# Moving the DRAM-to-DRAM copies of a strided slice to the gpsimd queue and dealing the loads to the sync and scalar queues

## Chip, cores and metric

The kernel runs on one core of one Trainium2 chip. The metric is the device time of one execution in microseconds (us), the median of several runs; less is better. A core has 16 DMA engines, which move all the data here. The engines that issue DMAs are SP (sync), ACT (scalar) and POOL (gpsimd); no engine computes anything in this kernel.

## The reference

The reference takes an array `x` of 32 batches, each 1024 rows of 512 float32 numbers, and returns every second row of the first 512 rows of each batch.

```python
batch, seq, dim = 32, 1024, 512
x = np.random.randn(batch, seq, dim).astype(np.float32)
start, stop, stride = 0, 512, 2
...
return x[:, start:stop:stride, :].astype(np.float32)
```

A row is 2,048 bytes. The result has 32 x 256 rows, so 16.78 MB are read from HBM and 16.78 MB are written to it.

## The kernel before, in words

The 256 output rows of a batch are split by parity: the 128 rows with an even number and the 128 with an odd number (`two`, line 14, gives one parity of two batches as a pattern of 128 x 2 x 512). One parity of each batch is copied straight from `x` to `out`, DRAM to DRAM; the other is loaded into an SBUF tile, `held` (128 partitions x 32 batches x 512 numbers), and stored from there. `apart` (line 8) says which parity of a batch goes the direct way: it is 1 for batches 0, 1, 4, 5 of a group of eight and 0 for batches 2, 3, 6, 7.

The batches are taken in four groups of eight (`groups`, line 30). For each group the loop at lines 36 to 41 issues four loads on SP (line 40) and four direct copies on ACT (line 41), by turns. A load takes two neighbouring batches, 512 KB. A direct copy takes two batches of the group that have the same parity (steps of 5 or 3 apart), 512 KB also. The values of `apart` make the load and the copy of one turn of the loop take opposite parities. Every load of a group adds 16 to that group's own semaphore, `loaded[g]`, when it has landed; every copy adds 16 to `done[1]`.

After all 16 loads, SP goes on with the stores (lines 42 to 46): for each group it waits until the four loads of the group have landed (line 43), then issues eight stores, one for each batch, 256 KB each (line 46), which add to `done[0]`. Last, SP waits for all 32 stores and all 16 copies (lines 47 and 48), and the kernel ends.

So SP's queue holds 16 loads and behind them 32 stores, ACT's queue holds 16 copies, and POOL issues no DMA. Nothing in the program orders the copies against the loads or stores; the order in a queue is the order of issue. There is no planner.

Of the kernel before, what the change touches and what calls it, by code (L numbers as in the profile page):

```python
# [3 lines left out]

EIGHT = 8


def apart(b):


    return 1 - (b >> 1 & 1)


def two(t, b, step, parity):

    return t[b : b + step + 1 : step].rearrange("b (p two) d -> two p b d", two=2)[parity]


def kernel(tc, x, start, stop, stride, out):

    nc = tc.nc
    src = x[:, start:stop:stride, :]
    B, rows, D = out.shape
    P = rows // 2
    sp, act = nc.sync, nc.scalar
    groups = range(0, B, EIGHT)  # L30
    with tc.tile_pool(name="io", bufs=1) as io:
        held = io.tile([P, B, D], x.dtype, name="held")
        with tc.tile_critical():
            loaded = [nc.alloc_semaphore(name=f"loaded{g}") for g in groups]
            done = [nc.alloc_semaphore(name=f"done{i}") for i in range(2)]
            for g in groups:
                for i, (b, step) in enumerate(((0, 5), (2, 5), (1, 3), (3, 3))):
                    b += g
                    at = g + 2 * i
                    sp.dma_start(held[:, at : at + 2], two(src, at, 1, 1 - apart(at))).then_inc(loaded[g // EIGHT], 16)  # L40
                    act.dma_start(two(out, b, step, apart(b)), two(src, b, step, apart(b))).then_inc(done[1], 16)
            for g in groups:
                sp.wait_ge(loaded[g // EIGHT], 16 * 4)
                for b in range(g, g + EIGHT):
                    to = out[b].rearrange("(p two) d -> two p d", two=2)[1 - apart(b)]
                    sp.dma_start(to, held[:, b]).then_inc(done[0], 16)
            sp.wait_ge(done[0], 16 * B)
            sp.wait_ge(done[1], 16 * (B // 2))


# [1 line left out]
_INS = ['x', 'start', 'stop', 'stride']  # L52
_OUTS = [((32, 256, 512), 'float32')]

_NUMBERS = {'start': 0, 'stop': 512, 'stride': 2}


def kernel(**inputs):
    import numpy as _np
    import concourse.bacc as _bacc  # L60
    import concourse.tile as _tile
    from concourse import mybir as _mybir
    from concourse.bass_utils import run_bass_kernel_spmd as _run

    nc = _bacc.Bacc("TRN2", target_bir_lowering=False, num_devices=1)  # L65
    arrays, args = {}, []
    for name in _INS:
        if name in _NUMBERS:
            args.append(_NUMBERS[name])
            continue  # L70
        a = _np.ascontiguousarray(inputs[name])
        if a.dtype.kind in "iu":
            a = a.astype(_np.int64)
        arrays[f"in_{name}_dram"] = a
        args.append(nc.dram_tensor(f"in_{name}_dram", a.shape, _mybir.dt.from_np(a.dtype), kind="ExternalInput").ap())
    for i, (shape, dtype) in enumerate(_OUTS):
        dt = _mybir.dt.from_np(_np.dtype(dtype))
        args.append(nc.dram_tensor(f"out_{i}_dram", shape, dt, kind="ExternalOutput").ap())
    with _tile.TileContext(nc) as tc:
        kernel(tc, *args)  # L80
    r = _run(nc, [arrays], core_ids=[0])
    got = tuple(r.results[0][f"out_{i}_dram"] for i in range(len(_OUTS)))
    return got[0]
```

## Time and profile before

| | |
|---|---|
| Median of 4 runs | 81.31 us (81.17 to 81.41) |
| The profiled execution's own time | 81.28 us |
| Its span, first to last instruction | 79.5 us |
| Loads on SP | 16 x 512 KB, 8.39 MB |
| Direct copies on ACT | 16 x 512 KB, 8.39 MB |
| Stores on SP | 32 x 256 KB, 8.39 MB |
| Bytes that the DMA engines moved | 25.17 MB, mean 317 GB/s |
| Busy time of the compute engines | POOL 0.2 us, four memsets of the program's frame |

The table's byte counts take a direct copy once, although it reads HBM and writes HBM. In the profile, q1 is SP's queue and q10 is ACT's: their bytes are those of loads plus stores, and of copies. A DMA packet of 2,048 bytes is one row on one of the 16 DMA engines; packets of 4 bytes are the semaphore updates that end a DMA on each engine. "Landing" is when the last of these updates has arrived. A view can be cut to a window of time, in us from the start of the span.

### The profile page before, as it was taken

How to read it: one execution, taken by the hardware profiler on the slowest of the kernel's cores; microseconds unless marked ns; L12 is line 12 of the kernel's file. 1: busy time of each engine (PE TensorE's matmuls, PEld its weight loads, DVE VectorE, ACT ScalarE, POOL GpSimd, SP SyncE). 2: the span in 40 equal slices, each digit the busy share in tenths (PEclk: the TensorE clock that was granted, in tenths of full speed). 3: DMA queues.
4: the chain of work that ended last, by engine and by line, in shares of the span. 5: the costliest groups of instructions: out<-in, count | busy, mean ns of one | idle time of the engine just before them, and what ended most of it. 6: DMA issues, size and time to landing. Idle time of an engine off the chain costs nothing. (4 is left out here: it accounts for less than half of the span.)

```text
span 79.5 us, 115 instructions
## 1 busy us (share of the span) xinstructions
POOL 0.2 (0%) x4
## 2 busy tenths in 40 slices
POOL 1000000000000000000000000000000000000000
DMA  0899989999999999999999999989999999999980
GB/s 0 250 311 279 282 257 351 339 341 373 326 322 366 352 332 310 299 292 304 364 356 341 355 349 308 301 239 406 407 403 389 351 346 361 344 362 362 347 277 9
DMA packets 13312, 25.17 MB, mean 317 GB/s; under 512 B 1024, under 2 KB 1024, under 8 KB 13312
## 3 DMA queue, kind: packets, MB, share of 16 engines
q1 hardware_dynamic: 8960, 16.78, 64.0%
q10 hardware_dynamic: 4352, 8.39, 32.6%
HBM read 16.78 MB, written 16.78 MB: 422 GB/s over the span
## 5 line engine op out<-in xcount | busy, mean ns | idle before, releaser
L65 POOL MEMSET const-bfloat16-1.0<- 128x1 bf16 x1 | 0.1, 101 | 0.0
L65 POOL MEMSET const-uint8-127<- 128x1 uint8 x1 | 0.1, 101 | 0.0
L65 POOL MEMSET const-float32-0.0<- 128x1 f32 x1 | 0.1, 98 | 0.2 <-issue 0.2
L65 POOL MEMSET const-float32-1.0<- 128x1 f32 x1 | 0.1, 98 | 0.0
## 6 DMA issues: line engine op xcount, KB each, us to landing
out_dram<-in_x_dram ACTq DMA_DIRECT2D x16, 512.0 KB, 22.2
held<-in_x_dram SPq DMA_DIRECT2D x16, 512.0 KB, 22.3
out_dram<-held SPq DMA_DIRECT2D x32, 256.0 KB, 10.1
```

The costliest lines, as they stand in the source:

```text
L65: nc = _bacc.Bacc("TRN2", target_bir_lowering=False, num_devices=1)
```

## The change

The direct copies are issued by POOL (`nc.gpsimd`) in place of ACT. The loads are dealt by turns to SP and ACT: the first and third of each group on SP, the second and fourth on ACT, eight on each queue in all. The stores stay on SP with their waits as they were, now behind eight loads in place of 16. Sizes, patterns, semaphores and the number of DMAs are the same.

```diff
-    sp, act = nc.sync, nc.scalar
+    sp, act, pool = nc.sync, nc.scalar, nc.gpsimd
...
                     at = g + 2 * i
-                    sp.dma_start(held[:, at : at + 2], two(src, at, 1, 1 - apart(at))).then_inc(loaded[g // EIGHT], 16)
-                    act.dma_start(two(out, b, step, apart(b)), two(src, b, step, apart(b))).then_inc(done[1], 16)
+                    to = held[:, at : at + 2]
+                    (sp, act)[i % 2].dma_start(to, two(src, at, 1, 1 - apart(at))).then_inc(loaded[g // EIGHT], 16)
+                    pool.dma_start(two(out, b, step, apart(b)), two(src, b, step, apart(b))).then_inc(done[1], 16)
```

## Prediction before the run

> **What bounds the kernel now.** I read the page first, for who is busy.
>
> ```profile
> span 79.5 us, 115 instructions
> ...
> DMA  0899989999999999999999999989999999999980
> GB/s 0 250 311 279 282 257 351 339 341 373 326 322 366 352 332 310 299 292 304 364 356 341 355 349 308 301 239 406 407 403 389 351 346 361 344 362 362 347 277 9
> ...
> q1 hardware_dynamic: 8960, 16.78, 64.0%
> q10 hardware_dynamic: 4352, 8.39, 32.6%
> HBM read 16.78 MB, written 16.78 MB: 422 GB/s over the span
> ...
> out_dram<-in_x_dram ACTq DMA_DIRECT2D x16, 512.0 KB, 22.2
> held<-in_x_dram SPq DMA_DIRECT2D x16, 512.0 KB, 22.3
> out_dram<-held SPq DMA_DIRECT2D x32, 256.0 KB, 10.1
> ```
>
> All 16 DMA engines are busy from 2 us to 77 us, and a DMA lands 10 to 22 us after its issue: it stands in line. So the issuing of DMAs is not the bound; the time is bytes over rate. But the rate isn't constant: about 320, then four slices at 389 to 407, then about 350. I cut the time at those places and asked for the windows (columns: window, its length, POOL's busy time and count, clock, DMA share, GB/s).
>
> ```profile
> 2.00:53.50 51.50, 0.00 (x0) 1.00 1.01 319
> 53.50:56.00 2.50, 0.00 (x0) 1.00 1.05 403
> 56.00:60.50 4.50, 0.00 (x0) 1.00 1.05 406
> 60.50:76.50 16.00, 0.00 (x0) 1.00 1.06 354
> ```
>
> The engines are equally busy in all four, so the slow windows are made of longer packets, not of gaps. Next, the queues' shares in the first window, and then in the first microsecond of the second.
>
> ```profile
> q1 hardware_dynamic: 4342, 8.39, 51.9%
> q10 hardware_dynamic: 4169, 8.05, 48.7%
> ```
>
> ```profile
> q10 hardware_dynamic: 103, 0.20, 52.7%
> q1 hardware_dynamic: 106, 0.19, 50.5%
> ```
>
> In the first, loads (q1) and copies (q10) share the engines equally; nearly every byte there is read from HBM, at 319 GB/s. In the second, copies still hold half, but q1 has gone from loads to stores (the last load was issued at 31.2 us and landed 23.4 us later, at 54.6; its bulk was over by 53.5): half of the bytes are read from HBM, all are written to it, and the rate is 403. The packet records say the same: before 53.5 a 2,048-byte packet usually takes 84 ns, but about one in thirteen takes 100 ns or more, up to 1,000 and over; from 53.5 to 60 all take 84, copies' too. From 60.5 on, with stores alone, about half take 90 to 150.
>
> So what costs time is reading at full rate. Copies beside stores ran at the engines' own rate; copies beside loads did not. Before, all reading is done first (16.4 MB, 51.5 us) and one half of the writing, the stores, is left over for a stage that reads nothing.
>
> **What the Trainium skill says.** "DMA: Bandwidth & Descriptors", section "Issuing engines are not separate DMA queues": DMAs of all issuing engines run on the same 16 engines, and using more engines saves only issue time. The trace agrees that issue time is not wanted. Its section "Queues, rings and completion order": each DMA engine takes its queues in turn, packet by packet. The 51.9% and 48.7% agree for two queues. Its section "SWDGE vs HWDGE vs iDMA": a DMA from GpSimd has its descriptors made by software on that engine and kept in SBUF, with a packet preferably up to 4,096 bytes; its "Latency and other measured facts" gives about 1 us to the first byte against 0.6, and says that DMA engines 7 and 15 are usually slower, perhaps because of these rings. No DMA in this trace is of that kind, so nothing here confirms it.
>
> **The change part by part.** Bytes, packets and semaphores stay the same: 8.39 MB each of loads, copies and stores.
>
> *Dealing the loads to two queues.* SP issued its loads unhindered up to the eighth (16 issues took 33.06 us because the queue was full). With eight loads each, SP and ACT issue theirs in 6 to 8 us and SP reaches the first wait. Behind the wait on SP are only stores. Issue time: nothing, hidden by the queued transfers; without that cover, eight issues of 0.4 to 2.0 us.
>
> *A third queue.* With three queues in turn the copies have a third of the engines while loads run, in place of a half. The loads end earlier, and a part of the copies is left to run beside stores. The first group's four loads are 2.1 MB, at two thirds of 319 GB/s some 10 us after the first packet, so SP's waits end long before its queue reaches stores: nothing waits there.
>
> Stage 1, loads and a third of copies: 8.39 / (2/3) = 12.58 MB, nearly all reads, at 319 GB/s: 39.4 us. Stage 2, the other 4.19 MB of copies beside as many bytes of stores: 8.39 MB. This mix is what stood at 403 GB/s for 2.5 us; the lower bound is the later stores' 354, if writing at over 400 can't be held (alone it fell to 354 after 60.5). So 20.8 to 23.7 us; I take 385 GB/s, nearer to the mix itself: 21.8. (Should copies get two thirds here, since a copy's packets are twice as many per DMA as a store's, stage 2 shrinks and stage 3 grows; the sum moves by under 1 us.) Stage 3, 4.19 MB of stores at 354: 11.8 us.
>
> Around them: 2.0 us to the first packet (SP still issues first). At the end, 5.90 MB at 354 from 60.5 would end at 77.2 and the last packet came at 77.9: 0.7 us for engines that end unequally. From there 1.6 us to the end of the span, and 1.8 from the span to the execution's time (81.28 - 79.5).
>
> Sum: 2.0 + 39.4 + 21.8 + 11.8 + 0.7 + 1.6 + 1.8 = 79.1 us, with 78.1 and 81.0 at the two rates of stage 2. The same stages for before are 2.0 + 51.5 + 24.4 (to 77.9) + 3.4 = 81.3, which is its own time, and the median is 81.31, 0.03 above it.
>
> *POOL as issuer.* POOL has 16 copies to issue after its memsets, which end at 0.43 us. The profile shows no such issue. From below, the skill's 1 us to the first byte per DMA: 16 us in all (estimate), hidden by 61 us of stages 1 and 2. From above, 61 / 16 = 3.8 us each would just feed them; more makes POOL the bound. I take it as hidden, since a copy on ACT took 0.64 us to issue unhindered and five times that is a lot. What a packet of the new kind costs on the DMA engine is unknown: it could be the same 84 ns, even less stalled (a deeper queue), or more. I take it as equal. Each extra ns on 4,096 packets over 16 engines is 256 ns in all.
>
> *ACT* loses 16 copies and gets eight loads; nobody waits behind them.
>
> **The rivals.**
>
> *Software-made packets are dearer* (slower). In place: the POOL queue on the DMA engines, the descriptors' fetch from SBUF, unequally on engines. The gain to be lost is 81.3 - 79.1 = 2.2 us. It decides from 2.2 us / 256 = 8.6 ns per copy packet (10% of 84), or from the slowest DMA engine being 2.9% (2.2 of 76 us) behind. At twice to three times that, 16 to 26 ns, the time is 79.1 + 4.1 to 6.7 = 83 to 86 us. For it: the skill's remarks on rings and engines 7 and 15, and that nothing of this kind is in the trace. Against: bytes and number of packets stay the same, and the skill names a tendency there, not a price.
>
> *Copies are starved and come last.* If a turn of POOL's queue is 2 rows and a turn of the others a whole DMA's 16, copies get 2 of 34 while loads run and 2 of 10 beside stores: 8.89 / 319 = 27.9, then 10.49 / 403 = 26.0 (at 354, 29.6), then 5.8 MB of copies alone at 319, 18.1. With the 6.1 around: 78.1 to 81.7. Faster too, but with POOL's queue last.
>
> *The share doesn't change* (no difference). If POOL's queue gets half against both load queues together, for instance by longer turns, all is as before: 81.3. Stage 1's rate would have to be the same too.
>
> *Two load streams and copies collide more.* Now SP's and ACT's loads always have opposite parities, and copies sit beside one of them. Stage 1 at 300 GB/s in place of 319 costs 41.9 - 39.4 = 2.5 us: 81.6. It would cancel the gain; loads alone, 2 to 3.5 us, ran slower, but that is the start.
>
> **How the numbers follow.** Faster with the third-share stages 0.40; faster with starved copies 0.08; no difference 0.07, which takes the unchanged share and cancelling costs; slower by dearer packets or POOL's issuing 0.33; slower by colliding reads 0.12. About 0.2% (0.16 us) is what a measurement of this kernel can tell from no change. So 0.48, 0.07, 0.45. The time is that of the first case, 79.1, its own range 77.5 to 81.0 (the upper rate everywhere beside stores gives 78.1, the last stores at 403 instead of 354 take off 1.4 in part). The whole range reaches up to 86, the upper end of the dear packets; above are POOL-bound cases (0.12), below 77.2 is 0.07.
>
> **What would show it.** After: a third queue with 8.39 MB; loads landed by about 41 us (before, 54.6); copies' last landing at about 63 us (before, 56.5), and a stretch from 41 to 63 us at over 380 GB/s; stores last, at 354. If copies land at 75 us or later, they were starved or POOL's issues were too slow (their spacing tells); if packets of POOL's queue are longer on average than the 100 ns of q10's now (32.6% of 79.5 us x 16 over 4,096), they are dearer; if the first stage is under 310 GB/s, reads collide. The forecast is wrong if copies beside stores run no faster than copies beside loads, for then 403 was an accident of that moment.

## The result, and the profile after

The changed kernel takes 81.82 us (median of 43 runs, 81.46 to 82.33) against 81.19 us before (64 runs, 80.72 to 82.26): a ratio of 1.0075, 95% interval 1.0061 to 1.0089. It is slower by 0.6 us; the forecast was 79.1 us, faster. The profiled execution took 81.92 us with a span of 80.2 us (before: 81.28 and 79.5). Ratios, here and below, leave out executions more than 1.5% above the fastest of their kernel, and can differ by up to 0.4% from the quotient of the medians, which are of all.

The page of the changed kernel has a third queue, q0, which is POOL's; q1 is SP's (half of the loads, all stores), q10 is ACT's (the other loads). In the last line, POOL's own issues: sixteen of 696 ns, 11.0 us in all.

```profile
DMA  0799999999999999989999999999999999999810
GB/s 0 210 314 306 313 251 364 320 337 344 356 349 342 371 327 382 332 316 316 296 267 342 342 305 396 400 347 361 406 407 386 352 348 358 358 352 352 292 46 0
...
q1 hardware_dynamic: 6784, 12.59, 47.8%
q0 software_dynamic: 2304, 8.39, 29.0%
q10 hardware_dynamic: 2176, 4.19, 17.0%
...
L42 POOL DMA_DIRECT2D out_dram<-in_x_dram x16 | 11.0, 696 | 1.0 <-PEq L80 1.0
```

The last slice has 0 GB/s, where before it had 9: the last data packet ended at 77.3 us (before, 77.9), so the transfers are over sooner than before and the kernel is not. Two more things are to be seen. q0 moved the same 8.39 MB as ACT's queue did before, but in 2,304 packets in place of 4,352: less the 256 semaphore updates, 2,048 packets of 4,096 bytes, two rows each. And their share of time, 29.0% of 80.2 us on 16 engines, is 372 us for 4,096 rows, 91 ns a row; before, it was 101 ns.

The windows of the changed kernel, cut where the mix of transfers changes (columns as in the prediction):

```profile
2.00:49.00 47.00, 10.50 (x16) 1.00 1.00 323
49.00:56.00 7.00, 0.00 (x0) 1.00 1.03 375
56.00:61.00 5.00, 0.00 (x0) 1.00 1.06 406
61.00:75.00 14.00, 0.00 (x0) 1.00 1.06 355
75.00:77.50 2.50, 0.00 (x0) 1.00 0.42 149
```

Loads and copies run to 49 us (the last load landed at 50.6, the last copy at 56.8, by the landing records), then copies beside stores to 56, then stores alone. Loads ended 4 us earlier than before (54.6), not the 14 that the forecast had (41). In most of the first window, 12 to 48 us, the queues shared the engines like this:

```profile
q0 software_dynamic: 1604, 5.85, 44.3%
q1 hardware_dynamic: 1605, 3.09, 29.6%
q10 hardware_dynamic: 1591, 3.07, 26.8%
```

Three queues, nearly the same number of packets each; with two rows in each of POOL's, the copies got 5.85 of 12.01 MB, 49%, nearly as with two queues.

Last, what SP waited for in the changed kernel:

```profile
SPq L33 <- DMA out_dram<-held: 10.1, 1, 10.1
SPq L33 <- POOLq L33: 1.2, 1, 1.2
```

The first line, the wait for the last stores, is the only one for line 33 before, and is 10.1 us there as well:

```profile
SPq L33 <- DMA out_dram<-held: 10.1, 1, 10.1
```

The second line of the changed kernel is new. Line 33 opens the section that holds all DMAs; at its end the engines that took part are gathered. The trace's instruction records show what POOL does there: a drain of 1,371 ns, begun after the last store's landing was seen. In the kernel before, POOL issues nothing in the section and isn't waited for at this place.

So the account between the two profiled executions is short. Last landing: 78.33 us before, 77.77 after, 0.56 earlier. From there to the end of the span: 1.17 us before, 2.38 after, 1.21 later. Together +0.65; the executions differ by 81.92 - 81.28 = 0.64.

### The profile page after: what moved, and what is told of

It reads as the page before. It is cut to its first block, busy times and chain, and to the rows that moved or that the text cites. A ratio compares the mean times of both kernels' runs of the same rounds, so it can differ in the third digit from the quotient of the medians.

```text
span 80.2 us, 117 instructions
## 1 busy us (share of the span) xinstructions
POOL 11.2 (14%) x20
## 3 DMA queue, kind: packets, MB, share of 16 engines
q0 software_dynamic: 2304, 8.39, 29.0%
## 5 line engine op out<-in xcount | busy, mean ns | idle before, releaser
L42 POOL DMA_DIRECT2D out_dram<-in_x_dram x16 | 11.0, 696 | 1.0 <-PEq L80 1.0
```

Source lines behind the costliest of these rows:

```text
L42: pool.dma_start(two(out, b, step, apart(b)), two(src, b, step, apart(b))).then_inc(done[1], 16)
```

## The experiments

Theory 1: POOL's drain at the end makes the kernel slower, and the transfers are slightly faster than before. Theory 2: the copies kept their half because queues take turns by packet and POOL's packets hold two rows. The rivals: the loss lies in the transfers; the share goes by queue and bytes. And the ground of the forecast, that copies beside stores run at about 400 GB/s, was to be tested by itself. Ratios are to the kernel before, run on the same chip beside each group of experiments.

### A drain behind the copies

```diff
+            pool.drain()
             for g in groups:
                 sp.wait_ge(loaded[g // EIGHT], 16 * 4)
```

> The changed kernel with one drain on POOL right behind its 16 copies. Theory 1 (the loss is POOL's drain after the last store, 1.37 us in the trace after, beside transfers that are not slower than before): the early drain waits while the stores still run, the one at the end falls below 0.1 us, and the time is 81.8 - 1.3 = 80.5 us, ratio to before about 0.99. Rival (a drain at the end costs POOL this much whenever it has issued DMAs, or the loss lies in the transfers): 81.8 us, ratio 1.007.

Measured: 79.90 us against 80.58, ratio 0.9923 (0.9897 to 0.9949). By its record the early drain took 48.8 us, from 8.3 us to 57.2, while stores ran; the one at the end took 41 ns. It ended 0.70 us after the last copy's landing (56.4), as in the three other runs below that drain early behind sixteen copies; behind eight it was 0.38 us. Those landings lay between 46.6 and 69.1 us and the 0.70 us was the same each time. So this drain waits for the landings and takes time after them, and it costs nothing here because the stores ran on for 20 us. SP's wait at line 33 has no part for POOL any more:

```profile
SPq L33 <- DMA out_dram<-held: 6.9, 1, 6.9
```

Theory 1 stands. One instruction that nobody waits for takes the changed kernel from slower than the one before to faster. From the last store's landing to the end of the span it is 1.18 us, as before (1.17), where the changed kernel has 2.38.

### The changed kernel again

> The changed kernel itself once more, beside the others on one chip, to set the early drain's gain against it and to see how far apart the last two stores land (1.5 us in its first trace, 0.8 in that of before). Ratio 1.0075 as before if the chip doesn't matter; the last drain on POOL 1371 ns again if it is a price per DMA, another value if it waits for something outside the program.

Measured, without any edit, on another chip than the early drain's: 81.00 us against 80.56, ratio 1.0058 (1.0029 to 1.0087); the last drain 1,371 ns again, to the nanosecond. The last store landed 1.4 us after the one before it. Against the early drain's 0.9923 the difference is 1.35% of 80.6 us, 1.1 us, where 1,371 - 41 ns were to be had. The last store landed at 76.92 us here and at 76.96 with the early drain, so in these two traces the difference lies behind the transfers.

### One copy, and eight copies, on POOL

The kernel before, with the first copy (below; or the first eight, in the second run) issued by POOL and counted on a semaphore of its own.

```diff
...
-                    act.dma_start(two(out, b, step, apart(b)), two(src, b, step, apart(b))).then_inc(done[1], 16)
+                    (act if g + i else pool).dma_start(two(out, b, step, apart(b)), two(src, b, step, apart(b))).then_inc(done[1 if g + i else 2], 16)
...
```

> The kernel before with its first copy alone moved from ACT to POOL, with a semaphore of its own. Theory 1 with a fixed price: POOL's drain at the end takes over 1 us even for one DMA issued 75 us earlier, and the time is 81.2 + 1.2 = 82.4 us. Theory 1 with a price per DMA (1.37 / 16 = 0.09 us): 81.3 us. Rival (no drain cost, transfers decide): 81.2 us.

Measured: 80.83 us against 80.58, ratio 1.0022 (0.9998 to 1.0046), not told apart from 1. The drain at the end took 137 ns.

> The kernel before with the first eight copies on POOL and the other eight on ACT. The drain at the end took 137 ns after one copy on POOL and 1371 after sixteen, so (1371 - 137) / 15 = 82 ns for each: 137 + 7 x 82 = 713 ns for eight. If it isn't linear (a table walked in blocks): 1371 or 137.

The only execution timed was the profiled one, 81.61 us, so there is no ratio; the drain took 717 ns. SP's wait for POOL in this run, to be set beside the 1.2 us for sixteen copies:

```profile
SPq L33 <- POOLq L33: 0.6, 1, 0.6
```

137, 717 and 1,371 ns for 1, 8 and 16 DMAs lie within 6 ns of a line of 82 ns for each with 55 over. So the price grows with what was issued on POOL and is paid at the first drain after it, even when all has landed 20 us before. All these DMAs were of 512 KB; whether DMAs, rows or packets are what counts was not tested.

### Copies to POOL, loads left on SP

```diff
-                    (sp, act)[i % 2].dma_start(to, two(src, at, 1, 1 - apart(at))).then_inc(loaded[g // EIGHT], 16)
+                    sp.dma_start(to, two(src, at, 1, 1 - apart(at))).then_inc(loaded[g // EIGHT], 16)
```

> Half of the change: the copies go to POOL, all loads stay on SP. Theory 2 (DMA engines take the queues in turn by packet, and POOL's packets hold two rows against one): with one load queue the copies get two thirds of the bytes, so their last landing is near 2 + 8.39 / (0.67 x 0.323) = 41 us plus the late start of about 4, and loads land last at 54 to 56 as before; the time is that of before plus POOL's drain, 82.5 us. Rival (the share is by queue and bytes): copies and loads end together at 54 to 57 us.

Measured: 81.90 us against 80.58, ratio 1.0159 (1.0129 to 1.0190). The last copy landed at 47.6 us (the one before it at 42.6), the last load at 56.0. The queues' shares from 12 to 40 us:

```profile
q0 software_dynamic: 1761, 6.43, 64.7%
q1 hardware_dynamic: 1761, 3.39, 36.4%
```

The same number of packets, to the packet, and 65% of the bytes for the copies. Theory 2 stands.

The same kernel with the early drain:

> All loads on SP, copies on POOL with the early drain behind them: the copies' move alone, without its price at the end. If the move to POOL is neutral for the transfers and the 0.8% by which the changed kernel with an early drain beats the one before comes from dealing the loads to two queues: time as before, ratio 1.00. If the move to POOL gives the gain (a copy packet took 90 ns per row there, 101 on ACT): ratio 0.992. If a single load queue lets the DMA engines end unequally, as in the same kernel without the early drain (its last store landed 2.2 us after the one before it): a ratio over 1.00.

Measured: 80.88 us against 80.46, ratio 1.0017 (0.9983 to 1.0052). The move to POOL alone gains nothing that the time shows; a gain came only with loads on two queues and the copies on a third. The traces show where this version loses against that one: the last store but one landed at 75.9 us (with loads dealt and the early drain, 75.8), the last one 2.6 us later (there, 1.2). Without the early drain it was 2.2 us. So the difference lies mostly in how unequally the DMA engines end, which the expectation named; but the profiled executions of these two versions were 0.5 us above their medians, so its size is uncertain, and no run tried it by itself.

### Loads dealt, copies left on ACT

The kernel before, with line 40's `sp` replaced by `(sp, act)[i % 2]`.

> The other half of the change alone: loads dealt to SP and ACT, copies left on ACT among its loads. If dealing the loads is by itself what made the transfers faster (0.992 with POOL and the early drain against 1.002 with all loads on SP): 0.99. If it needs a queue of its own for the copies, since ACT's loads now stand behind copies and SP's stores wait for them: loads land last at about 2 + 16.8 / 0.32 = 54 us or later, stores run beside copies at 325 to 375 GB/s, 1.01 to 1.04.

Measured: 83.18 us against 80.56, ratio 1.0290 (1.0223 to 1.0358). Loads landed last at 72.7 us, since ACT's loads stood behind copies in one queue, and SP stood at its four waits:

```profile
SPq L46 <- DMA held<-in_x_dram: 48.5, 4, 14.9
```

So neither half of the change made the kernel faster alone. This half isn't a clean test of dealing the loads, since here half of them stood behind copies, which they don't in the changed kernel.

### All loads first, copies behind them on ACT

Against the changed kernel: ACT issues the sixteen copies in a loop of their own behind its loads, and POOL issues nothing.

```diff
-                    pool.dma_start(two(out, b, step, apart(b)), two(src, b, step, apart(b))).then_inc(done[1], 16)
+            for g in groups:
+                for i, (b, step) in enumerate(((0, 5), (2, 5), (1, 3), (3, 3))):
+                    b += g
+                    act.dma_start(two(out, b, step, apart(b)), two(src, b, step, apart(b))).then_inc(done[1], 16)
```

> No POOL: loads dealt to SP and ACT, and ACT's 16 copies behind its loads, so that all copies run beside stores. It tests the ground of the forecast. If reading at full rate is what costs time and copies beside stores run at 403 GB/s: 8.39 MB of loads at 319 (26.3 us), 16.78 MB at 403 (41.6 us), with 2.0 + 0.7 + 3.4 around, 74.0 us. If the mix runs at 355 to 375, as in the trace after: 77 to 80 us. Rival (403 was an accident of that moment, and reading costs the same time wherever it lies): 81 us.

Measured: 83.89 us against 80.58, ratio 1.0425 (1.0372 to 1.0478). The windows: loads to 28 us, then copies beside stores, half and half, to 77.

```profile
2.00:28.00 26.00, 0.00 (x0) 1.00 1.00 320
28.00:33.00 5.00, 0.00 (x0) 1.00 1.05 398
33.00:77.00 44.00, 0.00 (x0) 1.00 1.01 323
```

Loads took what was forecast. The mix began at 398 GB/s, as in the trace of before, but kept it for 5 us and then ran 44 us at 323, no faster than copies beside loads. The packet records show who waits: from 40 to 76 us stores average 84 ns, copies 98 to 144 in each 4 us. The rival, that 403 was an accident of its moment, was right.

### The bytes split as the forecast had them

Against the version with the early drain: POOL issues copies 0 to 3 at once, then one pair when the first group's loads have landed, one when the second's have, and the last eight when all have.

```diff
+                    n = g // 2 + i
+                    if n in (4, 6, 8):
+                        pool.wait_ge(loaded[{4: 0, 6: 1, 8: 3}[n]], 16 * 4)
                     pool.dma_start(two(out, b, step, apart(b)), two(src, b, step, apart(b))).then_inc(done[1], 16)
```

> The changed kernel with the early drain, and POOL held back so that half of the copies lie beside all loads and half behind them: copies 0 to 3 at once, 4 and 5 when the first group's loads have landed, 6 and 7 after the second group's, 8 to 15 after the last loads. That is the split of the bytes that the forecast assumed. If the forecast's sum holds for that split: 79.1 / 81.3 = 0.973 of the time before, with loads ended near 41 us and the mix of copies and stores at 385 to 403 GB/s. If the mix holds 325 to 375 GB/s only, as in the trace after and with all loads first: 0.985 to 1.00, no better than the early drain alone (0.992).

Measured: 81.97 us against 80.56, ratio 1.0191 (1.0136 to 1.0245), with the split as wanted: the last load landed at 42.3 us.

```profile
40.00:44.00 4.00, 1.45 (x3) 1.00 1.04 399
44.00:50.00 6.00, 4.01 (x6) 1.00 1.09 228
...
52.00:67.00 15.00, 0.00 (x0) 1.00 1.01 342
```

The mix, 52 to 67 us, ran at 342 GB/s. Ahead of it lies something else: POOL issued its last eight copies from 42.6 to 48.0 us; up to 45 the stores, alone then, took 84 ns a packet, and from 45 to 49 they averaged 179 to 202 in each us. The first of those copies moved at 49. That muddies this run, so the split was made once more with the last eight copies on ACT, behind its loads, and counted on a semaphore of their own:

```diff
...
-                    if n in (4, 6, 8):
-                        pool.wait_ge(loaded[{4: 0, 6: 1, 8: 3}[n]], 16 * 4)
-                    pool.dma_start(two(out, b, step, apart(b)), two(src, b, step, apart(b))).then_inc(done[1], 16)
+                    if n in (4, 6):
+                        pool.wait_ge(loaded[{4: 0, 6: 1}[n]], 16 * 4)
+                    if n < 8:
+                        pool.dma_start(two(out, b, step, apart(b)), two(src, b, step, apart(b))).then_inc(done[1], 16)
             pool.drain()
+            for g in (2 * EIGHT, 3 * EIGHT):
+                for b, step in ((0, 5), (2, 5), (1, 3), (3, 3)):
+                    b += g
+                    act.dma_start(two(out, b, step, apart(b)), two(src, b, step, apart(b))).then_inc(done[2], 16)
...
```

> The forecast's split of the bytes once more, with no POOL issue in the middle: copies 0 to 7 on POOL (paced by the first two groups' loads, early drain behind them), copies 8 to 15 on ACT behind its loads. In the version with all copies on POOL, stores slowed to about 180 GB/s at 45 to 49 us, while POOL issued its last eight copies and before the first of them moved. If that issuing slowed the stores: no such stretch, all else alike, about 82.0 - 2.4 = 79.6 us, ratio 0.99. If the stores slow down there by themselves: the stretch stays, ratio 1.02. If the forecast's stages were right and only that stretch spoiled them: 0.973.

Measured: 81.54 us against 80.48, ratio 1.0111 (1.0037 to 1.0184). The stretch of slow stores is gone:

```profile
40.00:44.00 4.00, 0.00 (x0) 1.00 1.03 373
44.00:50.00 6.00, 0.00 (x0) 1.00 1.02 343
50.00:68.00 18.00, 0.00 (x0) 1.00 1.02 328
```

and the mix still runs at 343 and then 328. (The profiled execution took 82.40 us, 0.9 above the median; with 0.9 us taken off the last window alone it would still be under 350.) The forecast's schedule, met as nearly as could be, is slower than the kernel before, with no drain to pay. (It also ended less equally: its last store landed 2.4 us after the one before, the two before it 0.5 apart.)

### Other stores first; two queues for the stores

What is the fast stretch? In the kernel before, the second group's stores were put ahead of the first's (the loop over groups at line 42 runs over 8, 0, 16, 24, the first batches of the groups).

> The kernel before with the second group's stores ahead of the first's. It asks what the stretch at 403 to 406 GB/s was, on which the forecast rested. If it belongs to the first group's stores: stores begin at about 355 and the fast stretch moves to about 60 to 65 us. If it is what follows when loads end, whichever stores come: the fast stretch stays at 53.5 to 60.5 us. The time stays that of before, within 0.3 us, in both.

Measured: 80.49 us against 80.46, ratio 1.0018 (0.9991 to 1.0045). The stretch stayed in its place:

```profile
53.00:60.00 7.00, 0.00 (x0) 1.00 1.06 404
60.00:76.00 16.00, 0.00 (x0) 1.00 1.04 348
```

So it doesn't belong to those stores. In these traces such a stretch follows the end of the loads (in the changed kernel, at its full rate, the end of the copies), and with the forecast's split a second one follows the end of the copies (68 to 73 us, 405 and 391 GB/s).

Last, from the version with the early drain, stores dealt to SP and ACT, with ACT waiting as SP does:

```diff
+                act.wait_ge(loaded[g // EIGHT], 16 * 4)
...
-                    sp.dma_start(to, held[:, b]).then_inc(done[0], 16)
+                    (sp, act)[b % 2].dma_start(to, held[:, b]).then_inc(done[0], 16)
```

> The changed kernel with the early drain, and the stores dealt by turns to SP and ACT. If a second queue helps writing as it seems to help reading: the stage of stores alone, 355 GB/s, becomes faster, up to the 406 of its first microseconds, 1 to 2 us less than the 79.9 of the early drain alone. If that rate is set beyond the queues: same time within 0.3 us, the copies getting half in place of two thirds while stores run.

Measured: 79.93 us against 80.46, ratio 0.9922 (0.9895 to 0.9950), the same as with one queue for stores. Stores alone, 62 us on, ran at 356 GB/s:

```profile
60.00:62.00 2.00, 0.00 (x0) 1.00 1.06 407
62.00:75.00 13.00, 0.00 (x0) 1.00 1.06 356
```

The rate of stores alone was the same from two queues as from one (351 to 355). The changed kernel with the early drain is the fastest that was found, beside this one: 0.8% under the kernel before.

## Why the prediction was wrong

It forecast 2.2 us faster; it came out 0.6 us slower. The time lies in the stated range, but on the side that stood for dearer packets, which did not come about; that the range held it is luck. In the forecast's sum the last packet comes at 75.7 us and the end of the span 1.6 us later; in the profiled execution it came at 77.3 and the end 2.8 us later. So of 2.8 us missed, 1.6 lie in the transfers and 1.2 behind them. By its steps:

*Issue time costs nothing.* Right. POOL's sixteen issues took 0.69 us each and were over at 12.5 us (11.0 us in all, less than the 16 estimated "from below"); SP's and ACT's loads took 13.8 and 12.8 us to issue, not 6 to 8. It cost nothing, since all DMAs stood in line, as before.

*Stage 1's rate.* Right: 319 GB/s was used, 323 measured. The rival of colliding loads falls with it.

*"With three queues in turn the copies have a third of the engines while loads run."* Wrong, and this is where the expected gain went first. The turn goes by packets (1,604, 1,605 and 1,591 in the changed kernel, 1,761 and 1,761 with loads on SP alone), and a packet of POOL's queue holds two rows, so "bytes, packets and semaphores stay the same" was wrong for the packets of the copies: 2,048 in place of 4,096. The prediction itself quoted the Trainium skill, "DMA: Bandwidth & Descriptors", section "SWDGE vs HWDGE vs iDMA", for packets of preferably up to 4,096 bytes; the trace agrees, with 2,048 packets of 4,096 bytes. It used that size only in a rival, where it set two rows against a whole DMA of sixteen on the other queues; that rival, starved copies, falls by the equal counts. Two against one would have given half, and the rival "the share doesn't change", 81.3 us.

*"This mix is what stood at 403 GB/s for 2.5 us."* Wrong as a rate to plan with, and this is why the gain wouldn't have come with the share either. In the changed kernel the mix held 375 GB/s for 7 us. With all copies beside stores it held 398 for 5 us and 323 for the next 44; with the forecast's own split it was 328 to 343 in two runs, and the kernel 1.1% slower. A rate read from 2.5 us at a change of stages was stretched over 22 us, and its lower bound, 354, was taken from stores alone, which read nothing; the rate of the first stage, about 320, was the bound to take. The prediction's own sign of being wrong, copies beside stores no faster than copies beside loads, came true: 323 and 323. At 328 GB/s the forecast's stage 2 is 8.39 / 328 = 25.6 us in place of 21.8, and its sum 82.9.

*"0.7 us for engines that end unequally."* Too small. From 75 us on, 2.5 us at 149 GB/s are 0.37 MB; at 355 they would have taken 1.05 us and ended at 76.05, but the last packet came at 77.3: about 1.3 us.

*"From there 1.6 us to the end of the span."* Wrong, it was 2.8 us, and this decides the sign. The sum carried over the end of the kernel before. It costed POOL as an issuer and not as an engine that has to finish: with POOL taking part, the section ends with its drain, 82 ns for each of its DMAs of 512 KB. The early drain shows it: with that one instruction the ratio goes from 1.0075 (1.0058 in the second measurement) to 0.9923.

*Dearer packets*, the rival that ended slower, is wrong in its mechanism: 91 ns a row on POOL's queue, 101 on ACT's before. It made up most of the chance given to slower; the drain was in none of the cases.

What stays open is, first, why three queues, two of them for loads, move these bytes about 0.8% faster than two, when neither half of the change does so alone. Up to 49 us both profiled executions ran at 323 GB/s; from 49 to 56 us the one before ran at 321 and the changed one at 375. So the gain seems to lie where left-over copies ran beside stores. But that stretch varies: with the early drain it was 368, and in the kernel before with only the stores' order changed 349, and no run changed it alone. Open too is why rates rise to about 400 GB/s for some 5 us when loads or copies end and fall then, with stores alone to 348 to 356, and what of POOL's DMAs the 82 ns count.

Last, what slowed the stores at 45 to 49 us in one run stays open. That POOL's issuing did it is argued from the time alone, which fits in part (it began 2.5 us after the first of these issues), and from its absence when ACT issued those copies, which changed the mix as well. While POOL issued its sixteen copies in the changed kernel, from 2 to 12 us, the engines moved 279 GB/s, no less than before (277).

## What to carry to other kernels

Before an engine is given its first DMA, look at what the program does at the end with every engine that has taken part, and price that too; here a drain placed where nobody waits, with 20 us of other transfers behind it, took away a loss of 1.2 us. The share of a queue is worked out from the bytes in its packets, which the page shows as bytes over packets for each queue, and not from the number of queues. A rate seen for a few microseconds where one stage passes into another is no rate for a stage: ask for a window in which the same mix has held for long, and if there is none, take the slower neighbour as the bound.

## What the runs showed that was not expected

- A drain on POOL took 137, 717 and 1,371 ns after 1, 8 and 16 DMAs of 512 KB issued there, though all had landed long before; with an earlier drain behind those DMAs it took 41 ns.
- In the changed kernel POOL's first packet moved at 6.7 us, 5.2 us after the first issue began at 1.5; SP's first load, in the kernel before, was issued at 0.9 and moved at 2.0 us, ACT's first copy at 3.6.
- Packets of POOL's queue mostly took 159 ns for 4,096 bytes, against 84 ns for 2,048 on SP's and ACT's (medians): 5% less a row.
- Stores with nothing beside them dropped to about 185 GB/s for 4 us, beginning while POOL issued eight copies, in one run; the cause wasn't tried by itself.
